# Softmax-minus-one-hot backward pass: the middle blocks' stores as two row transfers each

## The chip, the cores and the metric

The kernel runs on one core of a Trainium2 chip. The metric is the device time of one execution in microseconds, as the median of several runs. The kernel before took 1263.8 us (median of 3 runs, 1263.55 to 1264.0).

## The reference

The inputs are logits of 8 x 1024 x 8192 in float32 and one label for each of the 8 x 1024 rows. The output is the softmax of each row, less 1.0 at the row's label:

```python
logits_max = np.max(logits, axis=-1, keepdims=True)
exp_logits = np.exp(logits - logits_max)
softmax = exp_logits / np.sum(exp_logits, axis=-1, keepdims=True)
...
one_hot[batch_idx, seq_idx, labels] = 1.0
return (softmax - one_hot).astype(np.float32)
```

So 268 MB are read and 268 MB are written, and each row needs a maximum, an exponential with its sum, and a scaling with one subtraction.

## The kernel before, in words

**Tiling.** The 8192 rows are cut into B = 32 blocks of 256 rows. In a block, partition p holds rows 2p and 2p + 1, numbered j = 0 and 1, so that a block is 128 partitions x 2 rows x 8192 floats. One row set of a block (one j) is 128 x 32 KB = 4.194 MB, and the whole block is 8.389 MB. In HBM the two rows of a partition lie one behind the other, so a whole-block transfer moves one run of 64 KB for each partition, while a row transfer moves one run of 32 KB and steps over the next 32 KB. The tile X has SLOTS = 3 slots of a block each; block b sits in slot b mod 3. Loads, work and stores all use this one buffer in place.

**Work on one block** (`work`, from line 237 on). For each of its two row sets t0 and t1, DVE takes the negated maximum (`row_max`, TENSOR_REDUCE m<-X) and ACT the exponential with its sum (`exponentials`, ACTIVATE X<-X,m). Then `finish` (line 166) runs on DVE: the reciprocal of the sum and one SCALAR_TENSOR_TENSOR X<-X,r,hot, which scales the row set and subtracts the one-hot bytes. ACT prepares these bytes in PSUM (`mark`, the tiles away and hot), two row sets ahead. The order on DVE is: maximum of t0, maximum of t1, finish t0, finish t1. `finished[t]` is the semaphore value that says that row set t is ready to be stored.

**Transfers.** All loads and stores are issued by SP, in program order, so they stand in one queue. The strings LOADS and STORES (lines 14 and 15) give the form for each block: "r" is two transfers, one for each row set, and "w" is one transfer of the whole block (PIECES, line 88). `store` (line 112) issues one transfer for each piece, and each waits for `finished` of the last row set that it holds: a whole-block store waits for t1, a row store for its own row set. The last block is stored in four quarter pieces. `load` (line 100) issues one transfer for each piece of block b, and each waits for those stores of block b - 3 that touch the same rows (`meets`), since they empty the slot.

**Order on SP** (lines 251 to 260). Three blocks are loaded ahead. Then for each block b comes its store and, after it, one load. After block EARLY = 3 the load is left out, and after block LATE = 27 two are issued, so between these the load behind the store of block b is that of block b + 2, whose slot was emptied by the store of block b - 1. The blocks stored whole are 3 to 27; the blocks loaded whole are 6 to 30.

Every operation is recorded through the helper `run` (line 72), so that almost all rows of the profile carry line 77 and are told apart by their tiles: X<-in_logits is a load, out_dram<-X a store. An operation that waits for several semaphores carries the last of them, and a wait instruction of its own on the issuing engine stands ahead for each of the others.

Of the kernel before, what the change touches and what calls it, by code (L numbers as in the profile page):

```python
# [11 lines left out]
LATE = 27  # L12

LOADS = "rrrrrrwwwwwwwwwwwwwwwwwwwwwwwwwr"
STORES = "rrrwwwwwwwwwwwwwwwwwwwwwwwwwrrrr"


@with_exitstack
def kernel(
# [45 lines left out]
    with tc.tile_critical():  # L65
# [46 lines left out]
        def store(b):  # L112
            stored[b] = []
            if b == B - 1:
# [8 lines left out]
                return  # L123
            for q, piece in enumerate(PIECES[STORES[b]]):
                ps, js = piece
# [168 lines left out]
```

## Time and profile before

| | |
|---|---|
| median of 3 runs | 1263.8 us |
| the profiled execution's own time | 1262.39 us |
| its span, from the first to the last instruction | 1260.6 us |
| moved by the DMA queues | 536.99 MB, 426 GB/s |
| share of SP's queue | 99.5% of 16 engines |
| DVE busy | 1120.2 us, 89% |
| ACT busy | 722.7 us, 57% |

The profile is of one execution. Its page gives busy times by engine, the DMA queues, the chain of work that ended last and the costliest groups of instructions. A group's row reads: line, engine, operation, the tiles written and read, shapes, count, then busy time in us and the mean of one in ns, then the idle time of the engine just before them and who ended it. The trace behind the page also answers for stretches of time (busy time of each engine, the DMA share and GB/s in each), for the order in time on one engine, and for who waited for whom. DMA packets are counted whole, so that the share and the rate of a short stretch can pass what is possible for a long one. SPq is SP's instruction queue, which issues the transfers.

### The profile page before, as it was taken

The page shows a single profiled execution, that of the slowest core. Times are in us where ns is not written, and L with a number is a line of the kernel's source. Part 1 is how long each engine was busy: PE and PEld are TensorE (multiplying, and loading weights), DVE is VectorE, ACT ScalarE, POOL GpSimd, SP SyncE. Part 2 cuts the span into 40 slices and gives each one's busy share as a digit, 9 for nine tenths or more (in the row PEclk, how much of TensorE's full clock was granted, in tenths as well). Part 3 has the DMA queues.
Part 4 walks back from the last instruction along what each step waited for, and adds up shares of the span by engine and source line. Part 5 has one row for each costly group of instructions (what it writes and reads, how often), then busy time and mean ns, then how long its engine had stood idle before and what let it go on. Part 6 is the DMA issues. An engine that isn't in the chain of part 4 may idle for free.

```text
span 1260.6 us, 747 instructions
## 1 busy us (share of the span) xinstructions
PE 0.4 (0%) x2; PEld 0.3 (0%) x2; DVE 1120.2 (89%) x208; ACT 722.7 (57%) x257; POOL 2.3 (0%) x7
## 2 busy tenths in 40 slices
PE   0000000000000000000000000000000000000000
PEld 0000000000000000000000000000000000000000
DVE  6899999688988889888898888988889888898995
ACT  3666676356655575545755547555475554755662
POOL 0000000000000000000000000000000000000000
DMA  9999999999999999999999999999999999999998
GB/s 401 416 433 433 434 448 433 430 433 430 433 430 433 433 420 416 430 433 433 416 443 406 433 433 433 412 420 433 433 433 401 430 433 433 433 433 400 435 432 368
DMA packets 11574, 536.99 MB, mean 426 GB/s; under 512 B 1296, under 2 KB 1296, under 8 KB 1328
## 3 DMA queue, kind: packets, MB, share of 16 engines
q1 hardware_dynamic: 11520, 536.88, 99.5%
q10 hardware_dynamic: 48, 0.07, 0.0%
q14 instruction: 6, 0.05, 0.0%
HBM read 268.50 MB, written 268.44 MB: 426 GB/s over the span
## 4 chain that ended last, share of the span: by engine, by line
DVE 50%; DMA 43%; issue 4%; ACT 2%; SPq 0%
DMA X<-in_logits_dram 43%; DVE X L77 25%; DVE m L77 25%; ACT X L77 1%; DVE r L77 1%; ACT hot L77 0%; SPq L77 0%; ACT away L77 0%; SPq L289 0%; SPq L65 0%
## 5 line engine op out<-in xcount | busy, mean ns | idle before, releaser
L77 DVE TENSOR_REDUCE m<-X 128x1 f32<-128x8192 f32 x64 | 553.0, 8680 | 114.3 <-DMA X<-in_logits_dram 114.3
L77 ACT ACTIVATE X<-X,m 128x8192 f32<-128x8192 f32 x64 | 455.8, 7122 | 308.6 <-DVE m L77 308.6
L77 DVE SCALAR_TENSOR_TENSOR X<-X,r,hot 128x8192 f32<-128x8192 f32 (+1 forms) x66 | 560.1, 8489 | 3.8 <-ACT hot L77 1.6
L77 ACT ACTIVATE away<-count,word 128x2048 bf16<-128x2048 int16 x64 | 128.1, 2001 | 199.1 <-DVE X L77 148.1
L77 ACT ACTIVATE hot<-away,unit,minus 128x2048 int32<-128x2048 bf16 x64 | 131.9, 2061 | 2.1
L77 DVE RECIPROCAL r<-s 128x1 f32<-128x1 f32 x64 | 9.9, 155 | 2.4 <-ACT X L77 2.4
L77 ACT ACTIVATION_READ_ACCUMULATOR X<-X,m 128x1 f32 x64 | 11.9, 186 | 0.0
L77 DVE CAST lab_f<-lab_raw 32x256 f32<-32x256 int32 x1 | 0.4, 372 | 4.9 <-DMA lab_raw<-in_labels_dram 4.9
L77 ACT ACT_TABLE_LOAD x1 | 1.3, 1283 | 3.2 <-POOL count L77 3.2
L77 POOL IOTA count<- 128x2048 int16 x1 | 1.8, 1823 | 0.0
L77 DVE TENSOR_TENSOR unit<-unit,part 128x64 f32<-128x64 f32 x3 | 0.7, 224 | 0.1
L77 DVE CAST lab<-hot 128x64 int32<-128x64 f32 x1 | 0.2, 225 | 0.5 <-PE hot L77 0.5
L77 DVE TENSOR_SCALAR part<-minus 128x64 f32<-128x64 f32 x3 | 0.6, 195 | 0.1
L77 PE MATMUL hot<-ident,lab_f 32*128 32x32 f32 x2 | 0.4, 302 | 5.3 <-DVE lab_f L77 5.3
L77 PEld LDWEIGHTS hot<-ident,lab_f 32*128 32x128 f32 x2 | 0.3, 196 | 5.3 <-DVE lab_f L77 5.3
L77 DVE TENSOR_SCALAR part<-lab 128x64 int32<-128x64 int32 x1 | 0.2, 196 | 0.0
L77 DVE TENSOR_SCALAR word<-part 128x64 f32<-128x64 int32 x1 | 0.2, 195 | 0.0
L77 DVE TENSOR_SCALAR lab<-lab 128x64 int32<-128x64 int32 x1 | 0.2, 195 | 0.0
L77 DVE CAST minus<-lab 128x64 f32<-128x64 int32 x1 | 0.2, 195 | 0.0
L77 DVE TENSOR_SCALAR unit<-minus 128x64 f32<-128x64 f32 x1 | 0.2, 195 | 0.0
L77 DVE TENSOR_SCALAR minus<-unit 128x64 f32<-128x64 f32 x1 | 0.2, 195 | 0.0
L77 POOL TENSOR_SCALAR_AFFINE_SELECT ident<-ident 32x32 f32<-32x32 f32 x1 | 0.2, 203 | 0.1
(5 smaller groups left out, 0.5 us busy)
## 6 DMA issues: line engine op xcount, KB each, us to landing
X<-in_logits_dram SPq DMA_DIRECT2D x14, 4096.0 KB, 19.4
out_dram<-X SPq DMA_DIRECT2D x12, 4096.0 KB, 29.5
out_dram<-X SPq DMA_DIRECT2D x4, 2048.0 KB, 12.2
out_dram<-X SPq DMA_DIRECT2D x25, 23.7
X<-in_logits_dram SPq DMA_DIRECT2D x25, 43.1
lab_raw<-in_labels_dram ACTq DMA_DIRECT2D x1, 64.0 KB, 4.0
```

What stands on the lines that cost most here:

```text
L77: instruction = getattr(engine, method)(**operands)
```

## The change

```diff
 LOADS = "rrrrrrwwwwwwwwwwwwwwwwwwwwwwwwwr"
-STORES = "rrrwwwwwwwwwwwwwwwwwwwwwwwwwrrrr"
+STORES = "rrrrrrrrrrrrrrrrrrrrrrrrrrrrrrrr"
```

The blocks 3 to 27 are now stored as blocks 0 to 2 and 28 to 30 already were: two transfers of 128 x 32 KB in the place of one of 128 x 64 KB. Row set 0's transfer waits for `finished[t0]` and row set 1's for `finished[t1]`, where the one transfer waited for `finished[t1]`. On SP, 25 store instructions become 50; row 0, row 1 and the load behind them keep the order that store and load had. The whole-block load of block b + 3 now finds two entries in `stored[b]` and waits for both. The instructions of DVE, ACT, PE and GpSimd are the same, in the same order.

## The prediction

> **What bounds the kernel now.** I began with the page: the span, the busy shares, the DMA rows, the queue rows and the chain that ended last.
>
> ```profile
> span 1260.6 us, 747 instructions
> PE 0.4 (0%) x2; PEld 0.3 (0%) x2; DVE 1120.2 (89%) x208; ACT 722.7 (57%) x257; POOL 2.3 (0%) x7
> ...
> DMA packets 11574, 536.99 MB, mean 426 GB/s; under 512 B 1296, under 2 KB 1296, under 8 KB 1328
> ...
> q1 hardware_dynamic: 11520, 536.88, 99.5%
> ...
> HBM read 268.50 MB, written 268.44 MB: 426 GB/s over the span
> ...
> DVE 50%; DMA 43%; issue 4%; ACT 2%; SPq 0%
> ...
> L77 DVE TENSOR_REDUCE m<-X 128x1 f32<-128x8192 f32 x64 | 553.0, 8680 | 114.3 <-DMA X<-in_logits_dram 114.3
> ```
>
> The queue of SP, which carries every load and store, had packets in work for 99.5% of what 16 engines can give; DVE is at 89%. The chain names DVE for half of the span, but the bytes cannot go faster than the queue takes them. The last row says that DVE sat idle for 114.3 us in front of its maxima, all of it for loads. So the first question for any edit here is whether it changes the bytes per microsecond. The second is whether it ever lets the queue run dry.
>
> For the steady part I took the timeline around one turn of the loop, then SP's own waits between 230 and 1095 us (the latter with the columns: us in total, times, longest).
>
> ```profile
> 430.06 0.43 SPq L77 DMA_DIRECT2D X<-in_logits_dram  x1
> ...
> 433.88 17.28 DVE L77 TENSOR_REDUCE m<-X 128x1 f32<-128x8192 f32 x2 [4.21 <-DMA X<-in_logits_dram]
> ...
> 451.26 8.75 DVE L77 SCALAR_TENSOR_TENSOR X<-X,r,hot 128x8192 f32<-128x8192 f32 x1
> ...
> 460.12 8.75 DVE L77 SCALAR_TENSOR_TENSOR X<-X,r,hot 128x8192 f32<-128x8192 f32 x1
> ...
> 468.89 0.33 SPq L77 DMA_DIRECT2D out_dram<-X  x1
> ...
> 469.27 0.43 SPq L77 DMA_DIRECT2D X<-in_logits_dram  x1
> ...
> 473.41 8.69 DVE L77 TENSOR_REDUCE m<-X 128x1 f32<-128x8192 f32 x1 [4.55 <-DMA X<-in_logits_dram]
> ```
>
> ```profile
> SPq L77 <- DVE X L77: 813.6, 21, 44.3
> ```
>
> Read it as a ring. A block lands at 433.9, DVE works on it until 468.87, SP then issues its store at 468.89 and a load at 469.27. The load of the next block, issued at 430.06, lands at 473.4, 4.1 us after those issues. So when store and load are issued, the queue holds about 4 us of work: little, but not nothing. SP itself waits only for DVE in this stretch, never for an earlier store.
>
> Last come the rates in stretches. The columns are the stretch, its length, busy time of PE, PEld, DVE, ACT and POOL, the clock, the DMA share and GB/s.
>
> ```profile
> 62.50:160.00 97.50, 0.00 (x0) 0.00 (x0) 97.29 (x18) 64.95 (x23) 0.00 (x0) 1.00 1.00 431
> 160.00:240.00 80.00, 0.00 (x0) 0.00 (x0) 69.75 (x13) 47.53 (x18) 0.00 (x0) 1.00 1.01 437
> 240.00:360.00 120.00, 0.00 (x0) 0.00 (x0) 107.83 (x19) 67.67 (x24) 0.00 (x0) 1.00 1.00 433
> 360.00:1140.00 780.00, 0.00 (x0) 0.00 (x0) 693.41 (x120) 449.46 (x160) 0.00 (x0) 1.00 1.00 427
> 1162.50:1230.00 67.50, 0.00 (x0) 0.00 (x0) 67.36 (x13) 42.81 (x17) 0.00 (x0) 1.00 1.00 434
> 549.50:588.75 39.25, 0.00 (x0) 0.00 (x0) 34.92 (x6) 21.70 (x8) 0.00 (x0) 1.00 0.99 427
> ```
>
> The first and the fifth stretch hold row transfers alone (4.194 MB each). The third and the fourth hold whole-block transfers (8.389 MB). The second holds both. The share is 1.00 everywhere, so the rates are what matters: 431 and 434 for rows, 433 and then 427 for whole blocks. In a turn of 39.25 us DVE works 34.92 us: it would be the next limit only 4.3 us further down.
>
> **The change part by part.** Blocks 3 to 27 are stored by 25 instructions now. After the change there are 50. Work on the engines, loads, buffers and the order on SP stay: row 0, row 1, then the load, where it was one store, then the load.
>
> *SP.* 25 more issues of 0.33 us (row at 468.89) are 8.3 us of SP time, and each whole-block load now waits for two stores' semaphores. SP waits 813.6 us in the middle alone. Row 0's issue falls into such a wait, after the first SCALAR_TENSOR_TENSOR (451.26 + 8.75 = 460.0). Row 1's comes where the whole store's was, at 468.89. The load behind it is not moved. Its added wait is for the store of the block before, whose transfer stands in front of a load that lands at 473.4. A whole-block load takes 8.389 MB / 433 GB/s = 19.4 us, so that store had landed by about 454, 15 us before it is asked for. Cost: nothing. Without that cover it would be 0.33 us a turn, 8 us in all.
>
> Two loads do wait for a store, and both keep cover. These are rows of SP's queue in the timeline, where a merged row spans the wait inside it.
>
> ```profile
> 160.57 32.95 SPq L77 DMA_DIRECT2D out_dram<-X  x2
> 198.86 0.34 SPq L77 DMA_DIRECT2D X<-in_logits_dram  x1
> ...
> 1098.78 23.30 SPq L77 DMA_DIRECT2D X<-in_logits_dram  x2
> ```
>
> The load of block 6 goes out at 198.86, when the store of block 3 has landed. The store of block 4, issued at 193.2 (160.57 + 32.95 less its own 0.33), is then still ahead of it, 19.4 us of work. The load of block 30 goes out at about 1122 (1098.78 + 23.30), behind the store of block 27, while the load of block 29 is still to run. A landing that moves by less than a microsecond is hidden by these.
>
> *When the bytes start.* Row 0 can start 8.9 us sooner (460.0 against 468.89). With the queue never dry that gains nothing: it only stands deeper in line. The queue's work ahead at the load's issue grows from about 4 us to about 4 us plus row 1 and what is left of row 0, but the load's place in line is unchanged, since the same bytes stand before it. What could be gained is bounded by the queue's idle share, 0.5% of 1260.6 = 6.3 us. That share includes the start and the end, where this change does nothing. I take 0.
>
> *The rate of the bytes.* 25 stores are 209.7 MB. At 433 GB/s they take 484.3 us. No row shows a row store beside whole-block loads, so I bound it by the stretches. At the best, rows run at 434 where whole blocks run at 427: 483.2 against 491.1, a gain of 7.9 us. At the worst, 431 against 437: 486.6 against 479.9, a loss of 6.7 us. The nearest pair, stretches of about 100 us with undisturbed flow, is the third stretch (433) against the mean of the row stretches by length, (97.5 x 431 + 67.5 x 434) / 165 = 432.2: 485.2 against 484.3, **a loss of 0.9 us**. I take this one: it agrees with a small price per transfer, 0.04 us each. The bounds differ by stage as much as by shape.
>
> A rule that speaks against the change: the Trainium skill, in "DMA: Bandwidth & Descriptors", section "Anatomy of one DMA — SWDGE (gpsimd) path", puts a fixed cost of about 2.0 us on each DMA, mostly the wait until its last byte is confirmed, though fitted on another issue path. Paid in series by 25 more transfers it would add 50 us, as an estimate. That would end at 1314. The trace speaks against its being paid in series: the row-only stretch at 62.5 to 160 runs at 431 GB/s, 9.73 us for each 4.194 MB, beside 433 for transfers of twice the size.
>
> *The sum.* 0 + 0 + 0.9. The profiled execution took 1262.4 us (span 1260.6, 1.8 around it); with the change 1263.3. The median of the runs shown is 1263.8, 1.4 above the profiled one. So the forecast is **1264.7 us**.
>
> **The rivals.**
>
> *Faster: the middle stretch gets its lost rate back.* Between 360 and 1140 us the kernel moves 427 GB/s where rows get 434 and the same whole blocks got 433 before. At 434 the 780 us would be 767.4, so 12.6 us are there to be won. If what costs them is the width of the transfers, the stores' half returns: 6.3 us, for 1263.8 - 6.3 + 0.9 = 1258.4. If it is the shallow queue of 4 us, then row 0's early issue cures it for loads too: 1263.8 - 12.6 + 0.9 = 1252.1. For it: the stretches with a deep queue (62 to 160, 1162 to 1230) run at 431 and 434. Against it: from 240 to 360 us the transfers are just as wide and DVE waits for loads in the same manner, and the rate is 433. So neither cause gives 427 by itself. Likeliest of this case: 1258.4.
>
> *Slower: rows write HBM more slowly in this mix.* A row store leaves out every second 32 KB of the output, and the other half follows one transfer later; in the middle such writes run beside whole-block reads. The place is the 25 stores; the price is the worst pair above, 437 to 431, 6.7 us plus nothing else: 1270.5. It decides when the stores' rate falls by over 0.5%, to below 430.8 GB/s (209.7 MB then take 2.5 us more). For it: the early row stretch is the slower of the two, 431. Against it: the last row stretch, mostly row stores, has the best rate of all long ones, 434.
>
> *Slower by far: each transfer pays its latency in series.* The chain of work in order of time begins with the one row load that finds an empty queue (start, length):
>
> ```profile
> 0.96 12.42 DMA X<-in_logits_dram
> ```
>
> It takes 12.42 us from issue to use, 2.7 more than the 9.73 of a row transfer in a full queue. If each of the 25 added transfers paid this, 67 us would come on top: 1263.8 + 67 = 1331. That needs a queue that stops between transfers, and the share of 1.00 in the row stretches shows none.
>
> That the change does not do what it says I exclude: SP's program has 50 row stores in the place of 25 and nothing else differs.
>
> **How the numbers follow.** The forecast, no change of rate beyond 0.9 us, has a chance of 0.41. The recovered rate has 0.27, the slower writes 0.30, the serial cost 0.02. 0.2% is 2.5 us, about what a measurement of this kernel can tell from no change; so faster is below 1261.3 and slower above 1266.3. The forecast lies within, and its own range is 1262.5 to 1267; some 0.04 of it lies above 1266.3, and about as much of the slower rival's mass lies below. This gives 0.27 faster, 0.40 same, 0.33 slower. Cases of both signs hold more than half, so the range takes in the likelier form of each: from 1255 (between the two forms of the faster rival) to 1270.5.
>
> **What would show it.** Right: the queue's share stays at 99.5%, packets rise by about 25 x 128 for the rows plus the small ones that close each transfer, the stretch from 360 to 1140 stays at 427 GB/s, DVE's idle time before loads stays near the 114 us of now, and row 0's issue comes about 8.9 us ahead of row 1's. The faster rival shows as 430 GB/s or more in that stretch and shorter waits of DVE for loads. The slower one shows as 424 or less there and longer waits. What would make the forecast wrong at its root is a load that waits on SP for a store in the middle, or a share clearly below 99%.

## The result, and the profile after

The changed kernel takes **1254.48 us** (median of 4 runs, 1253.49 to 1255.01) where the kernel before takes 1263.67 (4 runs, 1263.42 to 1264.0): a ratio of 0.9926, 95% interval 0.9911 to 0.9942. It is 9.2 us faster. The forecast was 1264.7 with a range from 1255 to 1270.5, so the time lies just outside, on the side that was thought less likely. A ratio in this document leaves out runs over 1.5% above the fastest of their kernel, which only the ninth experiment has.

The page of the changed kernel, in the rows that answer to those shown of before:

```profile
span 1251.7 us, 797 instructions
PE 0.4 (0%) x2; PEld 0.3 (0%) x2; DVE 1120.2 (89%) x208; ACT 722.7 (58%) x257; POOL 2.3 (0%) x7
...
DMA packets 15174, 536.99 MB, mean 429 GB/s; under 512 B 1696, under 2 KB 1696, under 8 KB 1728
...
q1 hardware_dynamic: 15120, 536.88, 99.6%
...
DVE 50%; DMA 42%; issue 4%; ACT 2%; SPq 0%
...
L77 DVE TENSOR_REDUCE m<-X 128x1 f32<-128x8192 f32 x64 | 553.0, 8680 | 104.6 <-DMA X<-in_logits_dram 104.6
```

The same work on every engine, the same bytes, 3600 more packets (25 x 128 for the rows and 25 x 16 small ones), and a queue that is as full as before: 99.6% for 99.5%. Only the mean rate differs, 429 GB/s for 426. DVE waits 9.7 us less for loads, 104.6 for 114.3.

The same stretches of the changed kernel (stretch, length, PE, PEld, DVE, ACT, POOL, clock, DMA share, GB/s):

```profile
62.50:160.00 97.50, 0.00 (x0) 0.00 (x0) 97.29 (x18) 64.94 (x23) 0.00 (x0) 1.00 1.01 433
160.00:240.00 80.00, 0.00 (x0) 0.00 (x0) 69.24 (x13) 47.51 (x18) 0.00 (x0) 1.00 1.00 430
240.00:360.00 120.00, 0.00 (x0) 0.00 (x0) 106.78 (x19) 67.67 (x24) 0.00 (x0) 1.00 1.00 432
360.00:1140.00 780.00, 0.00 (x0) 0.00 (x0) 700.74 (x121) 451.08 (x160) 0.00 (x0) 1.00 1.00 433
1162.50:1230.00 67.50, 0.00 (x0) 0.00 (x0) 67.39 (x12) 43.08 (x15) 0.00 (x0) 1.00 0.98 422
```

The gain is in one place: from 360 to 1140 us the rate is 433 GB/s where it was 427. That is 780 x (1 - 427 / 433) = 10.8 us. The span is 8.9 us shorter, so some 2 us are given back. The last stretch shows where most of it goes: 422 GB/s for 434, a DMA share of 0.98, and DVE busy for 67.39 of 67.50 us. The stores of the last blocks are ready only as fast as DVE finishes them, and a queue that got there sooner runs thin.

One turn of the loop in the timeline of the changed kernel:

```profile
655.61 9.19 SPq L77 DMA_DIRECT2D out_dram<-X  x2
...
664.92 0.73 SPq L77 DMA_DIRECT2D X<-in_logits_dram  x1
...
668.71 17.28 DVE L77 TENSOR_REDUCE m<-X 128x1 f32<-128x8192 f32 x2 [4.27 <-DMA X<-in_logits_dram]
```

Row 0's store goes out 9.19 - 0.33 = 8.9 us before row 1's, as forecast. Call the time from the first store's issue of a block until the next block's load is used the **lead**: it says how much work the queue still holds when new work arrives. Here it is 668.71 - 655.61 = 13.1 us. Before, it was 473.41 - 468.89 = 4.5 us. Single turns differ: over blocks 10 to 26 the median is 12.6 us (12.5 to 13.8), and 4.4 us (3.7 to 5.1) before. Where a block is loaded in two rows, the lead is counted to the use of the second. The load is issued as late as before, 3.8 us ahead of the landing.

### The profile page after: what moved, and what is told of

Read it like the earlier page. It is cut to its first block, busy times and chain, and to the rows that moved or that the text cites. A ratio compares the mean times of both kernels' runs of the same rounds, so it can differ in the third digit from the quotient of the medians.

```text
span 1251.7 us, 797 instructions
## 1 busy us (share of the span) xinstructions
PE 0.4 (0%) x2; PEld 0.3 (0%) x2; DVE 1120.2 (89%) x208; ACT 722.7 (58%) x257; POOL 2.3 (0%) x7
## 3 DMA queue, kind: packets, MB, share of 16 engines
q1 hardware_dynamic: 15120, 536.88, 99.6%
## 4 chain that ended last, share of the span: by engine, by line
DVE 50%; DMA 42%; issue 4%; ACT 2%; SPq 0%
DMA X<-in_logits_dram 42%; DVE X L77 25%; DVE m L77 25%; ACT X L77 1%; DVE r L77 1%; ACT hot L77 0%; SPq L77 0%; ACT away L77 0%; SPq L76 0%; SPq L289 0%; SPq L65 0%
## 5 line engine op out<-in xcount | busy, mean ns | idle before, releaser
L77 DVE TENSOR_REDUCE m<-X 128x1 f32<-128x8192 f32 x64 | 553.0, 8680 | 104.6 <-DMA X<-in_logits_dram 104.6
```

The lines of the kernel that those rows point to most:

```text
L77: instruction = getattr(engine, method)(**operands)
```

## The experiments

Two theories. **Depth**: the early issue of row 0 keeps the queue deeper, and a deep queue moves bytes faster, even where the shallow one never stopped. **Width**: 32 KB runs flow better than 64 KB runs. Each run is set beside the kernel before on the same chip; those medians were 1263.86, 1263.26 and 1263.55 us in the three sets. For most kernels stand the rows of one turn of the timeline, and the row of the stretch from 360 to 1140 us; the medians of the lead come in a table further down.

### 1. Rows, but both issued late

```diff
-                    nc.sync, [finished[b * G + js.stop - 1]], put[b % SLOTS][q], "dma_start",
+                    nc.sync, [finished[b * G + G - 1]], put[b % SLOTS][q], "dma_start",
```

> The changed kernel, but both row stores of a block wait for the second row set, so both go out where the one whole store went. Theory depth (row 0 going out 9 us earlier keeps more work in the queue, and that alone lifts the rate): the gain goes, 1262 to 1264 us, and 360 to 1140 us of the trace moves 427 GB/s. Theory width (32 KB runs in place of 64 KB, whenever they are issued): the gain stays, 1253 to 1256 us, 432 GB/s or more in that stretch.

Measured: 1265.07 us, ratio 1.001 (0.9998 to 1.0022).

```profile
625.09 0.81 SPq L77 DMA_DIRECT2D out_dram<-X  x2
626.00 0.93 SPq L77 DMA_DIRECT2D X<-in_logits_dram  x1
629.81 17.28 DVE L77 TENSOR_REDUCE m<-X 128x1 f32<-128x8192 f32 x2 [4.74 <-DMA X<-in_logits_dram]
```

```profile
360.00:1140.00 780.00, 0.00 (x0) 0.00 (x0) 692.87 (x120) 448.67 (x159) 0.00 (x0) 1.00 1.00 427
```

The lead is back at 4.7 us and the rate at 427, with the same narrow stores. The whole gain is in the early issue, and width is not the cause.

### 2. Whole stores, the second maximum left out

```diff
-            row_max(t1)
+            maxed[t1] = maxed[t0]
             exponentials(t1)
```

The exponential of the second row set takes the first one's maximum as its bias and waits for its own load.

> The kernel before, with whole-block stores, but the maximum of the second row set of each block is left out (its exponential takes the first row set's maximum). DVE then finishes a block some 8.7 us sooner, so each whole store goes out with about 13 us of work in the queue in place of 4. Theory depth: the gain appears without narrow runs, 1252 to 1256 us, 432 GB/s or more from 360 to 1140 us. Theory width: no gain, 1262 to 1264 us, 427 GB/s.

Measured: 1258.46 us, ratio 0.9952 (0.994 to 0.9965), between the two expectations.

```profile
606.88 0.17 DVE L77 RECIPROCAL r<-s 128x1 f32<-128x1 f32 x1 [7.34 <-ACT X L77]
...
624.71 0.33 SPq L77 DMA_DIRECT2D out_dram<-X  x1
...
630.36 8.69 DVE L77 TENSOR_REDUCE m<-X 128x1 f32<-128x8192 f32 x1 [5.68 <-DMA X<-in_logits_dram]
```

```profile
360.00:1140.00 780.00, 0.00 (x0) 0.00 (x0) 524.95 (x101) 448.90 (x160) 0.00 (x0) 1.00 1.00 429
```

The lead did not grow as expected: with a maximum less, DVE waits 7.34 us for the first exponential, and the lead is only 630.36 - 624.71 = 5.7 us, not 13. Its median is 5.3 us, about one more than before. This goes with 429 GB/s and a time 5.4 us lower, without any narrow store; it does not by itself rule out that the missing DVE work helped in another way.

### 3. Loads as rows too

```diff
-LOADS = "rrrrrrwwwwwwwwwwwwwwwwwwwwwwwwwr"
+LOADS = "rrrrrrrrrrrrrrrrrrrrrrrrrrrrrrrr"
```

(on the changed kernel)

> The changed kernel with the loads of blocks 6 to 30 as two row transfers too, so nothing but row transfers is left. Theory width: what is left of the loss in the loads goes too, 1250 to 1254 us. Theory depth: the queue was deep enough already, 1254 to 1256 us.

Measured: 1254.1 us, ratio 0.9917 (0.9903 to 0.993). DVE can now begin when a load's first row is there, and the lead, from the first row store to the landing of the load's second row, is 628.89 - 607.38 = 21.5 us:

```profile
607.38 9.20 SPq L77 DMA_DIRECT2D out_dram<-X  x2
...
628.89 8.69 DVE L77 TENSOR_REDUCE m<-X 128x1 f32<-128x8192 f32 x1 [1.31 <-DMA X<-in_logits_dram]
```

```profile
360.00:1140.00 780.00, 0.00 (x0) 0.00 (x0) 700.65 (x121) 450.93 (x161) 0.00 (x0) 1.00 1.00 432
```

This is no better than the changed kernel's 13 us. More depth brings nothing that can be seen here, though the rows of the loads may cost something as well.

### 4. Loads as rows, stores whole

The same edit on the kernel before.

> The kernel before, its whole stores kept, but the loads of blocks 6 to 30 as two row transfers. Theory width: half the bytes of the middle are narrow, as in the changed kernel, but the stores keep their 64 KB runs: 1254 if it is all the same which half is narrow, 1262 to 1264 if the stores are what matters. Theory depth: DVE can begin when row 0 has landed, some 9.7 us sooner, so the stores go out sooner and the queue is deep: 1252 to 1256 us.

Measured: **1250.26 us**, ratio 0.9887 (0.9872 to 0.9902), the fastest of all, 13.6 us under the kernel before.

```profile
615.21 0.34 SPq L77 DMA_DIRECT2D out_dram<-X  x1
615.59 0.91 SPq L77 DMA_DIRECT2D X<-in_logits_dram  x2
617.79 8.69 DVE L77 TENSOR_REDUCE m<-X 128x1 f32<-128x8192 f32 x1 [2.62 <-DMA X<-in_logits_dram]
627.48 8.69 DVE L77 TENSOR_REDUCE m<-X 128x1 f32<-128x8192 f32 x1 [1.00 <-DMA X<-in_logits_dram]
```

```profile
360.00:1140.00 780.00, 0.00 (x0) 0.00 (x0) 705.36 (x123) 453.18 (x163) 0.00 (x0) 1.00 1.00 433
```

DVE starts on row 0 about 9.7 us before row 1 has landed, so the whole store goes out with a lead of 627.48 - 615.21 = 12.3 us. Depth comes here from the load side. Beside the third kernel, on the same chip and differing only in the stores, it is 3.8 us faster: in a deep queue, row stores cost something.

### 5. Loads as rows, but used late

```diff
-            arrived = {w[0].name: w for piece, w in loaded[b] if meets(piece, (every, one[j]))}
+            arrived = {w[0].name: w for piece, w in loaded[b] if 6 <= b <= 30 or meets(piece, (every, one[j]))}
```

(on the fourth kernel)

> The fourth kernel (whole stores, loads of blocks 6 to 30 as two rows), but DVE begins a block only when both rows have landed, as before. Theory depth: the block is ready no sooner, the queue holds 4 us when the store goes out, and the gain of 13 us goes: 1262 to 1265 us, 427 GB/s from 360 to 1140 us. Rival, narrow loads: what helped was the 32 KB runs of the loads, 1250 to 1252 us.

Measured: 1263.32 us, ratio 0.9993 (0.9981 to 1.0005).

```profile
627.28 0.34 SPq L77 DMA_DIRECT2D out_dram<-X  x1
...
631.04 17.28 DVE L77 TENSOR_REDUCE m<-X 128x1 f32<-128x8192 f32 x2 [3.78 <-DMA X<-in_logits_dram]
```

```profile
360.00:1140.00 780.00, 0.00 (x0) 0.00 (x0) 694.05 (x120) 448.11 (x159) 0.00 (x0) 1.00 1.00 426
```

The same transfers as in the fourth kernel, a lead of 3.8 us, and all of the 13 us are gone. The shape of the loads was not it.

### 6. Half of the early issue

```diff
-            for i, c in enumerate(sides if t >= T - G else [slice(0, V)]):
+            for i, c in enumerate(sides if t >= T - G or (t % G and 3 <= t // G <= 27) else [slice(0, V)]):
...
+                ready = sides_done[b * G + 1][0] if 3 <= b <= 27 and js.stop == 1 else finished[b * G + js.stop - 1]
                 w = run(
-                    nc.sync, [finished[b * G + js.stop - 1]], put[b % SLOTS][q], "dma_start",
+                    nc.sync, [ready], put[b % SLOTS][q], "dma_start",
```

(on the changed kernel)

> The changed kernel, but in blocks 3 to 27 the last operation on the second row set is cut into two halves, and row 0's store waits for the first half: it goes out some 4.4 us ahead of row 1's in place of 9. Theory depth, graded: part of the gain, 1256 to 1261 us. Depth as a threshold that 4 us already pass: 1254 to 1256 us. If the early issue were not the cause: 1254.

Measured: 1259.09 us, ratio 0.9966 (0.9954 to 0.9977): about half of the gain.

```profile
622.92 4.72 SPq L77 DMA_DIRECT2D out_dram<-X  x2
...
630.85 17.28 DVE L77 TENSOR_REDUCE m<-X 128x1 f32<-128x8192 f32 x2 [3.57 <-DMA X<-in_logits_dram]
```

```profile
360.00:1140.00 780.00, 0.00 (x0) 0.00 (x0) 697.40 (x140) 450.69 (x160) 0.00 (x0) 1.00 1.00 429
```

A lead of 7.9 us (median 8.6) and a rate of 429. The effect is graded, as depth said.

### 7. All transfers whole, both maxima left out

```diff
-            maxed[t] = run(
-                nc.vector, arrived.values(), dve, "tensor_reduce",
...
-            )
+            maxed[t] = list(arrived.values())
...
-                nc.scalar, [maxed[t]], act, "activation",
+                nc.scalar, [zeroed] + maxed[t], act, "activation",
```

(on the kernel before; the tile m is set to zero once, and each exponential waits for its load alone)

> The kernel before with all its whole-block loads and stores, but both maxima of each block are left out (the exponentials take a bias of zero). A block is then ready about 25 us after it has landed in place of 35, so store and load go out with some 14 us of work in the queue. Theory depth: all of the gain and no price for narrow runs, 1248 to 1252 us, 433 GB/s in the middle. Rival, a mix of narrow and wide transfers is needed: 1258 to 1264 us.

Measured: 1251.55 us, ratio 0.9906 (0.9893 to 0.9919).

```profile
614.21 0.33 SPq L77 DMA_DIRECT2D out_dram<-X  x1
614.58 0.43 SPq L77 DMA_DIRECT2D X<-in_logits_dram  x1
627.84 7.12 ACT L77 ACTIVATE X<-X,m 128x8192 f32<-128x8192 f32 x1 [9.47 <-DMA X<-in_logits_dram]
```

```profile
360.00:1140.00 780.00, 0.00 (x0) 0.00 (x0) 354.93 (x82) 451.65 (x163) 0.00 (x0) 1.00 1.00 433
```

The very transfers of the kernel before, in the same order, with a lead of 13.6 us for 4.5. The rate is 433 for 427. No transfer needs to be cut for the gain; it needs the queue to be fed earlier.

### 8. All rows, stores late

The first experiment's edit on the third kernel.

> Loads and stores of the middle all as rows, but both row stores of a block wait for the second row set. The queue is deep through the loads, which let DVE begin sooner. If narrow stores cost some 4 us by their shape, as the third kernel beside the fourth suggests: 1253 to 1255 us. If it was row 0's early issue that cost them there: 1250 to 1251 us.

Measured: 1254.41 us, ratio 0.9926 (0.9915 to 0.9938).

```profile
360.00:1140.00 780.00, 0.00 (x0) 0.00 (x0) 701.34 (x121) 452.23 (x161) 0.00 (x0) 1.00 1.00 432
```

With the early issue taken away again, the price of row stores in a deep queue stays, some 4 us above the fourth kernel (1250.26). It belongs to the shape, not to the moment of issue.

### 9 and 10. The shape of the stores, in a deep queue

```diff
+            "h": [(slice(0, P // 2), rows), (slice(P // 2, P), rows)],
```

(on the fourth kernel, with "h" for blocks 3 to 27)

> The fourth kernel (loads of blocks 6 to 30 as rows, so the queue is deep), with each whole store of blocks 3 to 27 as two transfers of 64 partitions, whose runs stay 64 KB. If the 4 us that row stores cost in a deep queue are for the number of transfers: 1253 to 1255 us. If they are for the 32 KB runs: 1250 to 1251 us.

Measured: 1600.83 us (six runs, 1580.61 to 1620.58), ratio 1.2569 (1.2518 to 1.262), far outside both cases.

```profile
360.00:1140.00 780.00, 0.00 (x0) 0.00 (x0) 514.90 (x88) 334.25 (x118) 0.00 (x0) 1.00 0.99 322
```

Cutting the same bytes by partitions costs a quarter of the rate, at a DMA share of 0.99. The Trainium skill, in "SBUF — State Buffer", section "Door 1: The DMA port swizzle (why `[64,N]` ≈ `[32,N]`)", has 64 neighbouring partitions reach half of the ports that 128 reach; the fall fits that direction, though no run here looks at ports. So it says nothing on the number of transfers, because the edit changed far more than that.

```diff
+            if STORES[b] == "w":
+                for j in range(G):
+                    for i, cs in enumerate(sides):
+                        w = run(
+                            nc.sync, [finished[b * G + G - 1]], put[b % SLOTS][G * j + i],
...
```

(on the fourth kernel)

> The fourth kernel with each whole store of blocks 3 to 27 as four transfers of 16 KB runs, all issued when the block is ready. If the cost grows with the number of runs: 25 stores had 3200 runs, rows 6400 for 4 us more, quarters 12800 for some 12 us more, 1260 to 1264 us. If it is a step between whole and cut partitions: 1254 us. If narrow runs cost nothing: 1250 us.

Measured: 1259.34 us, ratio 0.9967 (0.9956 to 0.9978), 9.1 us above the fourth kernel. Rows cost 3.8 for 3200 more runs, quarters 9.1 for 9600 more: 1.2 and 0.9 ns a run. So the price grows with the number of runs, a little less than in proportion. By the times alone, runs and transfers are not told apart, since both grow together. The traces hold each packet's length besides: in the median 2.418 us for 64 KB, 1.213 for 32 KB and 0.611 for 16 KB. A 64 KB run cut in two thus takes 0.008 us more, and cut in four 0.026. With 16 engines, 3200 such cuts make 1.6 of the 3.8 us, and 5.2 of the 9.1. So a good part of the price is for the runs; the rest is not placed.

## Why the prediction was wrong, point by point

**What bounds the kernel: right.** The queue bounds it before and after, and DVE's wait for loads shrank by about what the span gained (9.7 and 8.9 us).

**SP: right.** No load in the middle waits for a store, and 25 more issues cost nothing that can be seen: with both rows issued late, the first experiment is 1.2 us above before, at the edge of its interval.

**When the bytes start: this step failed.** It said that with the queue never dry, row 0's earlier start "gains nothing: it only stands deeper in line", took 0, and bounded the gain by the idle share, 6.3 us. The middle alone gained 10.8 us, while the share stayed at 1.00. The bound was no bound: a packet counts as busy for as long as it takes, and what a shallow queue loses is lost while packets are counted as busy. In order of the lead (median of blocks 10 to 26, and its range), with the form of the middle's stores:

| kernel | lead, us | left on the first engine, us | stores | GB/s, 360 to 1140 us | time, us |
|---|---|---|---|---|---|
| 5, loads as rows, used late | 4.2 (3.7 to 5.3) | 1.1 (0.2 to 1.8) | whole | 426 | 1263.32 |
| 1, rows late | 4.3 (3.7 to 5.4) | 1.2 (0.2 to 1.7) | rows | 427 | 1265.07 |
| before | 4.4 (3.7 to 5.1) | 1.0 (0.3 to 1.8) | whole | 427 | 1263.67 |
| 2, one maximum left out | 5.3 (4.8 to 6.2) | 1.2 (0.4 to 1.6) | whole | 429 | 1258.46 |
| 6, half early | 8.6 (7.9 to 9.2) | 1.7 (0.5 to 3.9) | rows | 429 | 1259.09 |
| 4, loads as rows | 12.3 (12.3 to 12.5) | 8.1 (8.0 to 8.6) | whole | 433 | 1250.26 |
| 8, all rows, stores late | 12.4 (12.3 to 13.2) | 5.7 (4.7 to 8.9) | rows | 432 | 1254.41 |
| 10, stores in quarters | 12.5 (12.4 to 13.4) | 5.4 (3.9 to 9.1) | quarters | 431 | 1259.34 |
| changed kernel | 12.6 (12.5 to 13.8) | 6.4 (5.1 to 8.7) | rows | 433 | 1254.48 |
| 7, no maxima | 13.7 (13.5 to 14.5) | 7.5 (5.9 to 10.3) | whole | 433 | 1251.55 |
| 3, all rows | 21.3 (21.2 to 22.0) | 15.3 (13.8 to 18.7) | rows | 432 | 1254.1 |

With about 4 us the rate is 426 or 427, whatever the shape; with 12 us and more it is 431 to 433, by the shape; and 21 us bring no more. The third column is the time that the first of the 16 engines to finish still needs for the load ahead, when the block's first store is issued (median and range of the turns from 360 to 1080 us); the next paragraphs explain it.

**Where the lost time sits.** The traces hold the start, length and size of every DMA packet. Before, most 64 KB packets take 2.418 us. What the longer ones take beyond that is 11.5 us from 360 to 1140 us, as a mean of the 16 engines: about the whole loss. In the changed kernel, with 1.213 us for 32 KB, it is 2.0. Of the 11.5, 7.9 lie in the last packet of an engine's share of a store: 238 of these 320 packets take over 0.05 us too long, and in the changed kernel none does. Two stretches of the kernel before, the second with the end of a store, show as many bytes in 11% more packet time (the last two columns are the DMA share and GB/s):

```profile
440.00:445.00 5.00, 0.00 (x0) 0.00 (x0) 5.00 (x2) 2.40 (x1) 0.00 (x0) 1.00 0.97 419
445.00:450.00 5.00, 0.00 (x0) 0.00 (x0) 5.00 (x1) 4.81 (x2) 0.00 (x0) 1.00 1.08 419
```

The 16 engines drift apart. Before, they end their shares of one load within 0.5 us of each other up to 130 us, and 2.5 to 3.3 us apart from 390 us on. So when a store is issued, the last engine still has about 4 us of the load ahead of it, but the first has only the 0.3 to 1.8 us of the third column. In each of the first five kernels of the table, the stretched last packets of the stores end, in the median, 21.1 to 21.3 us after the block's first store is issued. An engine's share of these bytes takes 19.3 us at full length (8 packets of 2.418). As an estimate from these figures, an engine gets to a store's bytes no sooner than about 1.8 us after the issue, and one that has less left loses the difference.

The turns bear this out. Before, in the turn whose store is issued at 587.29 us, 14 engines have under 1.8 us left, and 14 last packets are stretched; at 626.01 us these are 2 and 4. The sixth kernel shows it within one run. Up to the turn at 504.58 us its first engine has 2.7 us or more left, and no last packet of a store is stretched; from 544.53 us on it has 0.5 to 1.8 us left, and 1 to 11 are stretched in each turn.

**The rate of the bytes: right in sign, too small.** It took a loss of 0.9 us for row stores. In a deep queue they cost 3.8 us (the third kernel beside the fourth). In the shallow one it is 1.2 us (the first experiment beside before). The bounds of -7.9 and 6.7 held for the shape alone.

**The rivals.** The shallow queue, cured by row 0's early issue for loads too, was on record with 1252.1, and it is what happened: 12.6 us to be won, 10.8 of them won in the middle, the price of the shape and the thinner end taken off. It was held down because the stretch from 240 to 360 us had the same wide transfers, the same waits and 433 GB/s. That argument was read too strongly. The lead was as short there, 3.6 to 4.7 us in the three turns from 270 to 360 us, but the engines ended a load only 1.4 to 2.3 us apart, so that the first of them still had 1.8 and 1.9 us left in two of the three. The range stopped at 1255, above this form of the rival; that the time came within 0.5 us of it is luck. The slower rival's mechanism, narrow writes, exists as well, and is outweighed. The serial rival did not show: in a deep queue 25 more transfers cost 3.8 us in all, not 50 or 67.

**What stays open.** That depth is the lever is shown by experiments 1, 4, 5, 6 and 7. That the engines furthest ahead run short is read from the packets; no experiment changed the drift by itself. Why the engines drift, why the lost time is counted in the last packet of the store, and where the rest of the row stores' 4 us lies, is not known.

## What to carry to other kernels

A DMA share of 100% does not say that the queue moves all it can: compare GB/s between stretches, and ask how much work the queue still holds, on the engine that is furthest ahead, when the next transfer is issued. Feed it earlier, by starting compute on the first half of a load or storing the first half of a result, and prefer the side where cutting the transfer costs least: here row loads with whole stores (1250.26 us) beat both kernels compared. Undo the early issue and the new shape one at a time before crediting either.

## What the runs showed of the hardware

The queue's rate depended on its depth without a gap in its busy share: 426 or 427 GB/s with about 4 us of work ahead, 431 to 433 with 12 us or more. The 16 engines of one queue, 0.5 us apart at first, drifted to about 3 us apart before and up to 7.1 us in the changed kernel. Stores cut into two sets of 64 partitions, one behind the other, took the middle from 433 to 322 GB/s; stores cut into four along the row kept 431:

```profile
360.00:1140.00 780.00, 0.00 (x0) 0.00 (x0) 698.05 (x121) 447.97 (x161) 0.00 (x0) 1.00 1.01 431
```
